# Ordering a two-layer diffusion kernel's instructions by a replay on a timeline of engine stages

## The chip, the cores and the metric

The kernel runs on one core of a Trainium2 chip. The metric is the device time of one execution in microseconds (us); lower is better.

## The reference, cut to what matters

Two layers over 256 latent tokens and 256 context tokens of width 1024. Each layer is a half-step SwiGLU, a token mixer, and another half-step SwiGLU, all modulated by nine vectors that come from the conditioning vector through one wide weight (`ada`). The even mixer is a bidirectional RWKV-7 recurrence over 12 heads beside a Fourier mix; the odd mixer is a convolution module beside pooling.

```python
def half_ffn(h, m, off, g, w_gu, w_down):
    y = modulate(h, g, m[off], m[off + 1])
    return h + 0.5 * m[off + 2] * swiglu(y, w_gu, w_down)

    def step(S, inp):
        rt, wt, kt, vt, kkt, bt = inp
        sk = jnp.einsum('bhij,bhj->bhi', S, kkt)
        S = S * wt[:, :, None, :] - sk[..., None] * bt[:, :, None, :] + vt[..., None] * kt[:, :, None, :]
        return S, jnp.einsum('bhij,bhj->bhi', S, rt)
```

## The kernel before, in words

The kernel computes everything on tiles with the channel on the 128 partitions. A product at full precision is split into high and low parts, three matmuls per tile (`mm3`, lines 195 to 197), or two where the moving operand holds both parts (lines 446, 447); VectorE and ScalarE split the weights (lines 190, 191).

The stages, with their place in the profiled execution:

- 0 to 405 us: setup and the first half feed-forward of layer 0 for both streams (`ffn`). The products of its start are ordered by hand (`manual_schedule`), nothing after it is.
- 405 to 858 us: the even mixer. `even_in` multiplies by the input weight, `shift` mixes neighbouring tokens. The heads are worked on in three groups, G0, G1 and G2. A group first has its `features` (decays and keys), then its `inverse` of 32x32 triangular blocks: a transpose on VectorE (line 697), 30 dependent pairs of a product and a subtraction on VectorE (lines 706, 708), two more transposes (713, 718), and two sets of 128 small matmuls (lines 727 and 738) which I call INV1 and INV2. Then its `chain` runs: eight dependent steps, each of which has a preparation that depends on nothing of the step before (products `pg`, lines 783 and 786, and transposes, line 805).
- While the chain of G0 runs, the features and the inverse of G1 run beside it; while that of G1 runs, those of G2; beside that of G2 runs the output projection (`fouriers`, `project_most`).
- 858 to 883 us: the rest of the projection (`project_last`). Then two feed-forwards (`half_ffn`, to 1080 and to 1265 us), the odd mixer (to 1400 us) and the last feed-forward.

Beside the chains lies a filler, `ada_wide` (lines 245 to 271): the modulation vectors of layer 1, in 18 blocks. A block loads four tiles `wraw` of 512 KB from a pool of four buffers, runs eight matmuls of 32 columns (line 260) into a bank called `ada`, then four transposes (line 268) and a reduction (line 269). Nothing in the even mixer needs its result. `drive(wide, PR[1 + g])` says how many of its pieces stand in the program beside a step of a chain.

No order of the work after the start is written out. The kernel is built by a tile scheduler: each engine works off one queue in order, and the scheduler, while it replays the program on a model of the machine, lays at each engine's queue whichever ready instruction has the best priority. The priority is the place in the program, moved by what the kernel asks: the filler's matmuls stand in `high_priority(-200)`, so they are taken when little else is ready. What is ready at which moment is the model's answer, so the model sets the order of each queue.

## Time and profile before

| what | value |
|---|---|
| median of three runs | 1593.63 us (1588.56 to 1593.87) |
| profiled execution, its own time | 1594.17 us |
| its span, first to last instruction | 1592.5 us |
| mean granted TensorE clock, share of full speed | 0.954 |
| TensorE (PE) busy | 1483.9 us, 93% |
| VectorE (DVE) busy | 1092.9 us, 69% |
| ScalarE (ACT) busy | 707.8 us |
| GpSimd (POOL) busy | 202.5 us |

Busy times are sums of the intervals in which an engine worked. Two engines can both be far from idle in the whole and each be the limit of some stage, so the table is only a start: a stage is read by itself, by the busy times in that stretch and by the chain of waits that crosses it. In rows of line 260 the trace holds two records for one matmul; eight records are four matmuls.

### The profile page before, as it was taken

How to read it: one execution, taken by the hardware profiler on the slowest of the kernel's cores; microseconds unless marked ns; L12 is line 12 of the kernel's file. 1: busy time of each engine (PE TensorE's matmuls, PEld its weight loads, DVE VectorE, ACT ScalarE, POOL GpSimd, SP SyncE). 2: the span in 40 equal slices, each digit the busy share in tenths (PEclk: the TensorE clock that was granted, in tenths of full speed). 3: DMA queues.
4: the chain of work that ended last, by engine and by line, in shares of the span. 5: the costliest groups of instructions: out<-in, count | busy, mean ns of one | idle time of the engine just before them, and what ended most of it. 6: DMA issues, size and time to landing. Idle time of an engine off the chain costs nothing.

```text
span 1592.5 us, 27107 instructions
## 1 busy us (share of the span) xinstructions
PE 1483.9 (93%) x10680; PEld 1207.1 (76%) x10680; DVE 1092.9 (69%) x1943; ACT 707.8 (44%) x1245; POOL 202.5 (13%) x293
## 2 busy tenths in 40 slices
PE   5999999999989979999898899999999986899997
PEld 3788888888877755445586788898888875888886
DVE  4799963334689688578365776667666499777764
ACT  3432222222454462542452655545554355555542
POOL 0000100000132141330211000000000066200000
PEclk9999999999999879899898999999999998799999
DMA  9766953332322124565531566665666432446663
GB/s 367 242 231 236 342 199 97 99 86 87 122 88 79 33 101 173 164 191 186 173 121 42 156 189 189 183 196 159 187 192 184 143 116 80 133 135 195 184 183 98
DMA packets 69312, 253.22 MB, mean 159 GB/s; under 512 B 8032, under 2 KB 11888, under 8 KB 64448
## 3 DMA queue, kind: packets, MB, share of 16 engines
q1 hardware_dynamic: 64592, 219.46, 44.1%
q0 software_dynamic: 4592, 32.03, 5.7%
q8 instruction: 84, 1.38, 0.4%
q14 instruction: 44, 0.36, 0.1%
HBM read 249.36 MB, written 2.10 MB: 158 GB/s over the span
## 4 chain that ended last, share of the span: by engine, by line
PE 79%; DVE 14%; ACT 3%; issue 2%; POOL 1%; DMA 1%; SPq 0%; POOLq 0%; DVEq 0%; ACTq 0%
PE gu L446 13%; PE down L446 7%; PE gu L447 7%; PE gu L195 6%; PE gu L196 6%; PE gu L197 6%; PE ada L260 4%; PE down L195 3%; PE down L196 3%; PE down L197 3%; PE down L447 3%; DVE wlo L191 2%; PE gu L1095 2%; DVE ocv L1068 2%; DVE oo L1068 1%
## 5 line engine op out<-in xcount | busy, mean ns | idle before, releaser
L190 ACT CAST whi<-wraw 128x1024 fp32r<-128x1024 f32 (+2 forms) x298 | 304.2, 1026 | 484.4 <-PE gu L196 150.6
L191 DVE TENSOR_TENSOR wlo<-wraw,whi 128x1024 fp32r<-128x1024 f32 (+2 forms) x298 | 356.2, 1199 | 203.3 <-ACT whi L190 196.1
L446 PE MATMUL gu<-yy,whi 128*128 128x512 f32 x960 | 333.9, 395 | 5.4 <-DVE yy L377 4.0
L447 PE MATMUL gu<-yy,wlo 128*128 128x256 f32 x960 | 264.2, 277 | 0.0
L446 PEld LDWEIGHTS gu<-yy,whi 128*128 128x128 f32 x960 | 179.2, 188 | 49.0 <-DVE yy L377 7.0
L447 PEld LDWEIGHTS gu<-yy,wlo 128*128 128x128 f32 x960 | 180.2, 188 | 1.0
L195 PE MATMUL gu<-yh,whi 128*128 128x512 f32 (+1 forms) x448 | 168.2, 377 | 6.2 <-ACT yh L375 4.3
L196 PE MATMUL gu<-yl,whi 128*128 128x512 f32 (+1 forms) x448 | 167.8, 375 | 0.0
L197 PE MATMUL gu<-yh,wlo 128*128 128x512 f32 (+1 forms) x448 | 167.3, 374 | 0.0
L446 PE MATMUL down<-hx,whi 128*128 128x512 f32 x462 | 160.3, 394 | 0.0
L447 PE MATMUL down<-hx,wlo 128*128 128x256 f32 x462 | 128.0, 277 | 0.0
L350 POOL TENSOR_TENSOR rs<-ms,mhalf 128x2 f32<-128x2 f32 (+1 forms) x9 | 10.9, 1209 | 815.9 <-DVE ms L347 625.5
L195 PEld LDWEIGHTS gu<-yh,whi 128*128 128x128 f32 x448 | 86.3, 193 | 24.1 <-ACT yh L375 5.6
L446 PEld LDWEIGHTS down<-hx,whi 128*128 128x128 f32 x462 | 86.6, 188 | 20.1
L281 DVE SCALAR_TENSOR_TENSOR adaj<-adaw,cb 128x1024 f32<-128x1024 f32 x80 | 97.7, 1222 | 5.7 <-DMA adaw<-in_adat_dram 4.6
L196 PEld LDWEIGHTS gu<-yl,whi 128*128 128x128 f32 x448 | 86.7, 194 | 15.1 <-DVE yl L377 1.0
L197 PEld LDWEIGHTS gu<-yh,wlo 128*128 128x128 f32 x448 | 86.7, 194 | 14.9 <-DVE wlo L191 0.8
L447 PEld LDWEIGHTS down<-hx,wlo 128*128 128x128 f32 x462 | 86.7, 188 | 0.0
L260 PE MATMUL ada<-wraw,ccs 128*32 128x512 f32 x288 | 74.1, 638 | 0.7 <-DMA wraw<-in_ada_dram 0.5
L384 DVE SCALAR_TENSOR_TENSOR hlat<-down,mc,hlat 128x256 f32<-128x256 f32 x67 | 32.4, 483 | 57.9 <-PE down L197 50.3
L196 PE MATMUL down<-hl,whi 128*128 128x512 f32 (+1 forms) x176 | 67.9, 386 | 0.0
L195 PE MATMUL down<-hh,whi 128*128 128x512 f32 (+1 forms) x176 | 67.9, 386 | 0.0
(362 smaller groups left out, 2760.2 us busy)
## 6 DMA issues: line engine op xcount, KB each, us to landing
wraw<-in_gu_dram SPq DMA_DIRECT2D x176, 512.0 KB, 3.9
wraw<-in_ada_dram SPq DMA_DIRECT2D x72, 512.0 KB, 4.5
adaw<-in_adat_dram POOLq DMA_DIRECT2D x28, 1024.0 KB, 6.1
wraw<-in_down_dram SPq DMA_DIRECT2D x56, 512.0 KB, 3.5
wraw<-in_win_dram SPq DMA_DIRECT2D x22, 512.0 KB, 3.5
wraw<-in_down_dram SPq DMA_DIRECT2D x24, 384.0 KB, 3.2
wraw<-in_down_dram SPq DMA_DIRECT2D x16, 448.0 KB, 3.3
wraw<-in_owin_dram SPq DMA_DIRECT2D x14, 512.0 KB, 3.5
```

The source lines that it names most:

```text
L190: nc.scalar.copy(hi[:, :k, :], raw[:, :k, :])
L191: (eng or nc.vector).tensor_tensor(out=lo[:, :k, :], in0=raw[:, :k, :], in1=hi[:, :k, :].bitcast(F32), op=ALU.subtract)
L195: mm(ps, lhsT=wh, rhs=xh, start=start, stop=False, **k)
L196: mm(ps, lhsT=wh, rhs=xl, start=False, stop=False, **k)
L197: mm(ps, lhsT=wl, rhs=xh, start=False, stop=stop, **k)
L260: nc.tensor.matmul(ps[32 * g:32 * g + 32, :], lhsT=self.cs[:, k, :], rhs=w[:, i, :], start=k < 4, stop=k >= 4, tile_position=(0, 32 * g), ...
L281: nc.vector.scalar_tensor_tensor(out=junk, in0=w[:, i, :], scalar=1.0, in1=self.cb[v], op0=ALU.mult, op1=ALU.mult, accum_out=self.mod[0, v ...
L384: nc.vector.scalar_tensor_tensor(out=h[v][:, k, :], in0=ps[:, n * T:n * T + T], scalar=gate[v][:, k:k + 1], in1=h[v][:, k, :], op0=ALU.mul ...
L446: mm(ps, lhsT=wh, rhs=x.rearrange("p s t -> p (s t)"), start=start, stop=False, skip_group_check=True)
L447: mm(ps[:, :T], lhsT=wl, rhs=x[:, 0, :], start=False, stop=stop, skip_group_check=True)
L1068: nc.vector.scalar_tensor_tensor(out=c, in0=u[:, w:w + T], scalar=cw[:, j, w:w + 1], in1=c, op0=ALU.mult, op1=ALU.add)
L1095: nc.tensor.matmul(ps[k // 2][:, k % 2 * T:k % 2 * T + T], lhsT=a[:, k, :], rhs=b[:, q, :], start=first and n == 0 and k % 2 == 0, stop=la ...
```

## The change

The kernel sets one environment variable before the framework is imported. The scheduler then replays the program on another model, a timeline of engine stages, and orders the queues by what is ready there. The program, its instructions, its tiles and its buffers stay the same; each line number grows by 3.

```diff
--- before.py
+++ after.py
@@ -1,6 +1,9 @@
+import os
 from contextlib import ExitStack
 
 import numpy as np
+
+os.environ["CONCOURSE_TILE_TIMELINE_SIM"] = "all"
 
 import concourse.bass as bass
 from concourse import mybir
```


What it does to the queues shows in their order. Three places follow. Line numbers are each kernel's own; `x2` and the like count equal neighbours.

TensorE at the first inverse, that of G0. `down_4493` is a product of `even_in`; `misc_4124` to `misc_4229` are INV1 and INV2 (lines 727 and 738 before, 730 and 741 after); `ada` is the filler. Before:

```order
L197 MATMUL down_4493<-yh_2979,wlo_4488 128x256
L727 MATMUL misc_4124<-Dt_4116,A_3319 32x32 x32
L727 MATMUL misc_4159<-Dt_4116,A_3319 32x32 x32
L195 MATMUL down_4493<-yh_2979,whi_4487 128x256
L196 MATMUL down_4493<-yl_2980,whi_4487 128x256
L197 MATMUL down_4493<-yh_2979,wlo_4488 128x256
L195 MATMUL down_4493<-yh_2979,whi_4487 128x256
L196 MATMUL down_4493<-yl_2980,whi_4487 128x256
L738 MATMUL misc_4194<-A_3319,R_716_4123 32x32 x32
L738 MATMUL misc_4229<-A_3319,R_716_4123 32x32 x32
L197 MATMUL down_4493<-yh_2979,wlo_4488 128x256
```

After:

```order
L271 MATMUL ada_5235<-cst,adas_5233 128x128 x4
L263 MATMUL ada_5241<-wraw_5242,ccs 32x512 x2
L263 MATMUL ada_5241<-wraw_5246,ccs 32x512 x2
L263 MATMUL ada_5241<-wraw_5492,ccs 32x512 x2
L263 MATMUL ada_5241<-wraw_5496,ccs 32x512 x2
L271 MATMUL ada_5502<-cst,adas_5500 128x128 x4
L730 MATMUL misc_4124<-Dt_4116,A_3319 32x32 x32
L730 MATMUL misc_4159<-Dt_4116,A_3319 32x32 x32
L263 MATMUL ada_5508<-wraw_5509,ccs 32x512 x2
L263 MATMUL ada_5508<-wraw_5572,ccs 32x512 x2
L263 MATMUL ada_5508<-wraw_5576,ccs 32x512 x2
L741 MATMUL misc_4194<-A_3319,R_716_4123 32x32 x32
```

What remained of `even_in` stood around INV1 and INV2; now `even_in` is finished earlier, and blocks of the filler stand there, together with the first preparations of the chain of G0.

TensorE in the chain of G1, beside the inverse of G2. `mx_7231` and `down_7279` are steps of the chain, `pg_7311` a preparation. Before:

```order
L869 MATMUL mx_7231<-ar_4561,Xs_7130 64x64
L869 MATMUL mx_7231<-rs_7019,Xs_7130 64x64
L260 MATMUL ada_6958<-wraw_6967,ccs 32x512
L824 MATMUL down_7279<-XV_7163,AG_7180 64x64 x8
L786 MATMUL pg_7311<-ar_4561,bk_4557 128x128 x2
L786 MATMUL pg_7311<-ar_4561,bk_4558 128x128
L833 MATMUL down_7290<-RH_7288,A_4563 64x64 x8
```

After:

```order
L872 MATMUL mx_7231<-ar_4561,Xs_7130 64x64
L872 MATMUL mx_7231<-rs_7019,Xs_7130 64x64
L827 MATMUL down_7279<-XV_7163,AG_7180 64x64 x8
L789 MATMUL pg_7311<-ar_4561,bk_4557 128x128 x2
L789 MATMUL pg_7311<-ar_4561,bk_4558 128x128 x2
L789 MATMUL pg_7311<-ar_4561,bk_4559 128x128 x2
L789 MATMUL pg_7311<-ar_4561,bk_4560 128x128 x2
```

The filler's lone matmuls between the pieces of the chain are gone from here. In the whole kernel the 144 filler matmuls stood in 59 runs of neighbours, and now stand in 35. Counted in rounds of up to four neighbours there were 67 and are 48. The table says where they stand, with the number of chain steps and of preparations in the same stretch:

| stretch of the program | filler matmuls, rounds before | after | steps before, after | preparations before, after |
|---|---|---|---|---|
| inverse of G0 | 0, 0 | 30, 10 | 0, 0 | 0, 4 |
| features of G1 | 14, 6 | 32, 12 | 3, 4 | 5, 2 |
| inverse of G1 | 34, 14 | 50, 17 | 5, 4 | 7, 5 |
| features of G2 | 38, 18 | 32, 9 | 3, 3 | 1, 3 |
| inverse of G2 | 42, 21 | 0, 0 | 5, 5 | 7, 3 |
| chain of G2 | 16, 8 | 0, 0 | 8, 8 | 5, 7 |

TensorE at the start of the second feed-forward. `gu_8628` is a product with the raw rows, `misc_8543` spreads the reciprocal norm over the partitions, `gu_8670` and its like are the first products with the normalised rows `yy`. Before:

```order
L196 MATMUL gu_8628<-yl_8449,whi_8622 128x258
L197 MATMUL gu_8628<-yh_8448,wlo_8623 128x258
L446 MATMUL gu_8670<-yy_8454,whi_8664 128x512
L447 MATMUL gu_8670<-yy_8454,wlo_8665 128x256
L446 MATMUL gu_8670<-yy_8454,whi_8664 128x512
L447 MATMUL gu_8670<-yy_8454,wlo_8665 128x256
L446 MATMUL gu_8693<-yy_8454,whi_8687 128x512
L447 MATMUL gu_8693<-yy_8454,wlo_8688 128x256
L446 MATMUL gu_8693<-yy_8454,whi_8687 128x512
L447 MATMUL gu_8693<-yy_8454,wlo_8688 128x256
```

After:

```order
L198 MATMUL gu_8628<-yh_8448,whi_8622 128x258
L199 MATMUL gu_8628<-yl_8449,whi_8622 128x258
L200 MATMUL gu_8628<-yh_8448,wlo_8623 128x258
L449 MATMUL gu_8670<-yy_8454,whi_8664 128x512
L450 MATMUL gu_8670<-yy_8454,wlo_8665 128x256
L449 MATMUL gu_8693<-yy_8454,whi_8687 128x512
L450 MATMUL gu_8693<-yy_8454,wlo_8688 128x256
L449 MATMUL gu_8726<-yy_8454,whi_8720 128x512
L450 MATMUL gu_8726<-yy_8454,wlo_8721 128x256
L449 MATMUL gu_8749<-yy_8454,whi_8743 128x512
L450 MATMUL gu_8749<-yy_8454,wlo_8744 128x256
```

Two accumulators were worked on in turn, now four; and the spread, which stood 43 rows ahead of the first `yy` product, stands 12 ahead, behind most of the raw products. At the next feed-forward it moves from 45 rows ahead to 21, at the last from 45 to 1.

On SyncE, which issues the loads, the order is nearly the same. On VectorE, the 60 dependent operations of an inverse have others between them: 18 before and 25 after in G0, 45 and 41 in G1, 45 and 27 in G2.

## Rows read from the trace of the kernel before

**Rows 1.** The page: busy time of each engine, share of the span, instructions.

```profile
PE 1483.9 (93%) x10680; PEld 1207.1 (76%) x10680; DVE 1092.9 (69%) x1943; ACT 707.8 (44%) x1245; POOL 202.5 (13%) x293
```

**Rows 2.** The page: the chain that ended last, by engine and by line.

```profile
PE 79%; DVE 14%; ACT 3%; issue 2%; POOL 1%; DMA 1%; SPq 0%; POOLq 0%; DVEq 0%; ACTq 0%
PE gu L446 13%; PE down L446 7%; PE gu L447 7%; PE gu L195 6%; PE gu L196 6%; PE gu L197 6%; PE ada L260 4%; PE down L195 3%; PE down L196 3%; PE down L197 3%; PE down L447 3%; DVE wlo L191 2%; PE gu L1095 2%; DVE ocv L1068 2%; DVE oo L1068 1%
```

**Rows 3.** Busy by stretch: length, PE, PEld, DVE, ACT, POOL, clock, DMA, GB/s.

```profile
443.00:492.00 49.00, 41.51 (x446) 33.95 (x446) 42.80 (x62) 27.70 (x44) 19.82 (x34) 0.90 0.18 60
492.00:545.60 53.60, 50.93 (x496) 45.35 (x495) 42.60 (x91) 20.56 (x29) 4.17 (x12) 0.90 0.25 77
545.60:593.40 47.80, 39.29 (x601) 27.43 (x599) 38.73 (x65) 29.31 (x54) 23.92 (x37) 0.84 0.25 85
593.40:644.50 51.10, 49.19 (x584) 29.59 (x582) 44.27 (x114) 15.48 (x38) 7.31 (x11) 0.92 0.51 173
644.50:706.70 62.20, 57.14 (x847) 30.77 (x848) 36.62 (x67) 30.89 (x54) 23.90 (x32) 0.86 0.50 157
706.70:761.30 54.60, 50.56 (x572) 27.57 (x572) 43.35 (x112) 16.53 (x38) 7.88 (x12) 1.00 0.62 198
761.30:858.00 96.70, 90.95 (x1134) 70.15 (x1135) 50.47 (x104) 41.45 (x83) 19.37 (x23) 0.93 0.37 117
858.00:883.00 25.00, 19.62 (x98) 13.72 (x98) 13.92 (x34) 10.43 (x22) 3.48 (x4) 0.73 0.36 108
```

**Rows 4.** The same view for line 260 alone: length, PE, PEld, clock, DMA, GB/s.

```profile
545.60:593.40 47.80, 5.91 (x28) 1.06 (x28) 0.84 0.25 85
593.40:644.50 51.10, 15.43 (x68) 2.20 (x68) 0.92 0.51 173
644.50:706.70 62.20, 22.65 (x78) 3.15 (x80) 0.86 0.50 157
706.70:761.30 54.60, 21.59 (x84) 3.11 (x84) 1.00 0.62 198
761.30:858.00 96.70, 8.48 (x32) 1.28 (x32) 0.93 0.37 117
```

**Rows 5.** Timeline of PE, end of the third inverse; start, us, engine, line, tiles.

```profile
751.17 1.04 PE L260 MATMUL ada<-wraw,ccs 128*32 128x512 f32 x2
...
757.29 1.06 PE L260 MATMUL ada<-wraw,ccs 128*32 128x512 f32 x8
...
761.35 0.82 PE L727 MATMUL misc<-Dt,A 32*32 32x32 f32 x40 [2.99 <-DVE Dt L718]
```

**Rows 6.** Groups by line, TensorE, 545 to 858 us: preparations of a chain step.

```profile
L786 PE MATMUL pg<-ar,bk 64*128 64x128 f32 x192 | 26.7, 323 | 0.0
...
L805 PE MATMUL mx<-cst,bk 128*128 128x128 f32 x84 | 17.4, 313 | 1.0 <-ACT UV L775 1.0
```

**Rows 7.** Timeline of VectorE, then of TensorE: first inverse.

```profile
490.31 1.96 DVE L697 STREAM_TRANSPOSE Y<-A 128x1024 f32<-128x1024 f32 x1
...
530.99 1.96 DVE L718 STREAM_TRANSPOSE Dt<-Z 128x1024 f32<-128x1024 f32 x1
...
533.00 3.30 PE L727 MATMUL misc<-Dt,A 32*32 32x32 f32 x128 [1.83 <-DVE Dt L718]
```

**Rows 8.** The page, DMA issues: median us from issue to landing; x72.

```profile
wraw<-in_ada_dram SPq DMA_DIRECT2D x72, 512.0 KB, 4.5
```

**Rows 9.** The chain of waits in features of group 1: start, us, what.

```profile
560.90 3.82 DMA wraw<-in_ada_dram
```

**Rows 10.** Timeline of TensorE, first feed-forward into the even mixer.

```profile
402.94 0.36 PE L195 MATMUL gu<-hh,whi 128*128 128x256 f32 x1
405.49 0.38 PE L356 MATMUL misc<-cst,rs 128*128 128x128 f32 x2
407.38 0.50 PE L195 MATMUL down<-yh,whi 128*128 128x256 f32 x2 [1.51 <-ACT yh L375]
```

**Rows 11.** Timeline of TensorE, start of the second feed-forward.

```profile
892.26 0.69 PE L356 MATMUL misc<-cst,rs 128*128 128x128 f32 x2 [1.38 <-POOL rs L350]
```

## The prediction, made before the changed kernel had run

> **What bounds the kernel now.** I read the page from the top, then the chain that ended last, then the busy times by stretch, and last the timelines of the places where the order changes. TensorE is busy for 93% of the span [rows 1], and the chain runs through it for 79% and through VectorE for 14% [rows 2]. So most of the kernel is a queue of products on TensorE. The feed-forwards are dense, and a new order of dense work can only touch their starts. The filler of the even mixer is different: it is on the chain for 4% [rows 2], some 64 us, though nothing near it needs its result. A new order can make that work cheaper or put it into idle time.
>
> The stretches show where idle time is [rows 3]. From 443 to 492 us TensorE works 41.51 of 49.00 us, from there to 545.6 us 50.93 of 53.60 us: 10.2 us idle. In the features of G1 (545.6 to 593.4) 8.5 us are idle. In the two inverses (593.4 to 644.5, 706.7 to 761.3) only 1.9 and 4.0 us are, and 15.4 and 21.6 us of TensorE's time there go to the filler [rows 4]. The reader is to see that the filler is done mostly where TensorE has little to spare.
>
> The price of the filler depends on its neighbours. A lone matmul of it takes 1.04 us, and four that stand together take 1.06 us [rows 5]: they write four column groups. The unit is therefore a round of up to four, at 1.05 us, not a matmul. The five stretches check this: the sum of their times, 74.1 us [rows 4], over 67 rounds is 1.1 us each.
>
> **The change, stage by stage.** No instruction is added or removed, so each term is idle time, shared rounds, or work that changes places. The counts are those of the table in the section on the change. Besides rounds, preparations of a chain step move. One has eight `pg` products, at 26.7 us for 24 preparations, and transposes, at 17.4 us for 21 [rows 6]: with the smaller products about 2.2 us, an estimate.
>
> *To the end of the first inverse, +11 us.* Ten rounds come here (10.5 us) and four preparations (8.8 us). The 10.2 us of idle time can take half of that. I add 2 us for filler tiles that have not landed when TensorE comes to them: a load takes 4.5 us from issue to landing [rows 8], and the first four blocks ask for sixteen. 10.5 + 8.8 + 2 - 10.2 is +11. The inverse itself runs on VectorE, 42.6 us from its first transpose to the end of its last [rows 7], and TensorE waits 1.83 us for it ahead of INV1. If all of the new work fits beside VectorE the term is near 0; if the idle time can't be filled it is +21.
>
> *Features of G1, 0.* Six rounds more (+6.3), three preparations fewer (-6.6). One chain step comes in, for which 8.5 us of idle time are there. Range -5 to +6.
>
> *Inverse of G1, -3 us.* Three rounds more (+3.2), two preparations fewer (-4.4), one step gone (about -2, taken near a preparation's 2.2). TensorE is full here [rows 3], so this is on the path. Range -5 to +2.
>
> *Features of G2, -8 us.* 18 rounds took 22.65 us [rows 4]; nine at 1.05 take 9.5 us: -13. Two preparations more: +4.4. TensorE is busy 57.1 of 62.2 us, so nearly all of it counts. Range -12 to -2.
>
> *Inverse of G2, -9 us.* All 21 rounds leave (-21.6), and four preparations (-8.8). TensorE would be left with about 20 of its 50.6 us, and then VectorE is late next: the inverse's dependent operations. The stretch is 54.6 us long; the inverse of G0, with 18 foreign operations between its dependent ones, took 42.6 us [rows 7]. So -12 is the most. With 27 foreign operations I take -9. If VectorE's operations are spaced by something else than TensorE's answers, 0.
>
> *Chain of G2, -4 us.* Eight rounds leave (-8.5), two preparations come (+4.4). TensorE is busy 91.0 of 96.7 us. Range -8 to 0.
>
> These give -13 us. The filler's cover is then gone from the last two stretches: what was hidden under it, the waits of the chain for VectorE and ScalarE, appears; that is why I gave these two less than TensorE's own account.
>
> *First feed-forward into the even mixer, +2.5 us.* Before, 21 products stand between the statistics and their spread, from 402.94 to 405.49 us, and still 1.51 us are waited for `yh` [rows 10]. Now the last statistics come after nearly all of these products. The cover of 2.5 us is lost. Range 0 to +4.
>
> *Starts of the feed-forwards, -3 us.* TensorE waits 1.38 us for the reciprocal norm, with raw products left that don't need it [rows 11]. They now go first, here and at the next feed-forward: twice -1.4. At the last one the spread moves behind all raw products, which can undo it; I take 0. Range -6 to +3.
>
> *The clock, +1.5 us.* The granted clock was 0.84 where TensorE was busy 39.29 of 47.80 us, and 1.00 where it was busy 50.56 of 54.60 [rows 3]. The inverse of G2 would become the emptier kind. About 20 us of work at 0.84 cost 3.8 us more than at 1.00; half of it lies under VectorE's time. The Trainium skill, "TensorE: Matmul & The Clock Gate", Part 1, states that the slow clock is the default and activity releases the full one, which speaks against a change that empties TensorE; the rows agree, and by that rule the whole stretch could fall to 1.2 GHz, which is the third rival below.
>
> *The odd mixer, 0.* The order on GpSimd and VectorE changes a little there; I found no wait that it removes, and bound it by -3 and +5.
>
> **Sum:** -13 + 2.5 - 3 + 1.5 = -12 us. Against the profiled execution's 1594.2 us that is **1582 us**. The median shown, 1593.6 us, is 0.6 us lower, which I leave out. 0.5%, 8 us, is about what a measurement of this kernel can tell from no change: faster means below 1585.6, slower above 1601.6.
>
> A second rule bears on the rounds. The rows show that a lone round between 64x64 products costs as much as one of four, 1.04 and 1.06 us. The Trainium skill, "TensorEngine Tiling (Array Packing)", Key Properties, states that changing the tiling mode drains TensorE. By that rule runs would count, 59 before and 35 now: at 74.1 us over 59, 1.26 us each, 24 fewer would give 30 us instead of 19 rounds times 1.05, 20 us; the sum would be 10 us lower, inside the range.
>
> **The rivals.** *VectorE sets the pace (about 1592 us).* The path of the even mixer from one inverse to the next is then the string of dependent operations on VectorE, and TensorE's saved rounds become waits. For it: VectorE is busy 44.27 of 51.10 us in the inverse of G1. Against it: TensorE is fuller, 49.19 us. Price: the work that moves ahead of the first inverse costs nothing then, and both later inverses give nothing. What stays is half of the -8 in the features of G2, some of the -4 in the last chain, and +1 of the other stages: 1594 - 2. It decides where the third inverse stays above some 52 us.
>
> *The filler is fed too slowly (about 1605 us, the slower side).* The 72 loads now are wanted between the first inverse and the features of G2, some 155 us instead of 250, and only four buffers exist. A matmul that waits for its tile holds TensorE's queue, and the chain step behind it. That this can happen is seen once: 3.82 us of the chain of waits is such a load [rows 9]. If six of the 18 blocks wait that long, it is +22.9 us: 1605. It decides from 12 us on, 0.7 us per block, and from 20 us, 1.1 per block, it would be seen as slower. For it: 18 blocks of 2.1 MB in 155 us are 244 GB/s, beside 60 to 77 GB/s of others, where these stretches had 198 at most [rows 3]. Against it: four buffers of 512 KB that land in 4.5 us [rows 8] could carry 466 GB/s. If each block waited 3.82 us it were +69 us; I hold that unlikely, since the filler is late only while it outruns its loads.
>
> *The clock falls (about 1588 us).* With the filler gone after the features of G2, TensorE goes through the inverse half idle, and the chain of G2 begins at 0.73, a mean between the levels of 1.2 and 2.4 GHz, as in the stretch from 858 to 883 us, which was 25.00 us long and 19.62 busy [rows 3], instead of 0.93. Over 20 us of work that is 20 x (0.93 / 0.73 - 1), +5.5 us.
>
> *The setting does nothing.* The order shows that it does; no chance.
>
> **How the numbers follow.** Forecast 0.58, own range 1563 to 1590 (the terms' bounds, not all at one end at once). VectorE 0.12, clock 0.08, slow feed 0.17, other 0.05. Faster: 0.52 of the forecast, 0.02 of the clock, 0.02 of the others: 0.56. Slower: 0.13 of the slow feed, 0.05 of VectorE, other mishaps and the early +11 growing to +21, 0.02 of the forecast's upper bounds and 0.01 of the clock: 0.21. The same: 0.23. The range takes the forecast's and most of the rivals' times: 1560 to 1606.
>
> **What would show it.** Line 263, which is line 260 now, should be busy near 50 us instead of 74.1, and not at all in the second half of G2's inverse. The first inverse should end about 11 us later, the third inverse be some 43 to 47 us long. In the chain of waits the filler's share should fall, and no piece of more than 1 us should be a load of `wraw` more than twice. It is wrong if the filler's busy time falls and the even mixer still ends at 858 us (VectorE), or if TensorE's idle time is released by loads of `wraw`.

## The result and the profile after

The changed kernel is slower by 0.6%: 1602.76 us, median of 12 runs (1590.58 to 1605.64), against 1590.72 us (12 runs, 1582.56 to 1594.99); ratio 1.0059, 95% interval 1.0041 to 1.0077 (the two medians are 0.8% apart). The forecast was 1582 us. The profiled execution took 1604.17 us (span 1602.5), 10.0 us more than that of before.

The page of the kernel after, busy times [rows 1] and the chain that ended last [rows 2]:

```profile
PE 1468.3 (92%) x10680; PEld 1209.1 (75%) x10680; DVE 1096.4 (68%) x1943; ACT 710.0 (44%) x1245; POOL 202.1 (13%) x293
...
PE 64%; DVE 17%; issue 14%; ACT 2%; DMA 1%; POOL 1%; SPq 0%; DVEq 0%; POOLq 0%; ACTq 0%
```

TensorE works 15.6 us less than before, as the change promised, and the kernel takes 10 us more. So about 26 us of waiting are new. Where they lie is seen with the same landmarks in both kernels: the spread of a reciprocal norm at the start of each stage.

| stretch | before | after | difference |
|---|---|---|---|
| start to the spread of the second feed-forward (end of the even mixer) | 892.26 | 889.12 | -3.14 |
| from there to the spread of the odd mixer (two feed-forwards) | 381.68 | 383.59 | +1.91 |
| odd mixer, to the spread of the last feed-forward | 126.01 | 136.42 | +10.41 |
| from there to the end of the execution | 194.22 | 195.04 | +0.82 |
| sum | 1594.17 | 1604.17 | +10.00 |

Single executions vary by some us in each line. The profiles of the experiments below show by how much, where a version leaves the order of a stage as it was. The even mixer ended at 885.9 and 892.3 us in the old order and between 886.5 and 893.7 us (five profiles) in the new one; the means are 889.1 and 889.6, so over such profiles there is no gain. The odd mixer's loss is beyond the variation, but its size is not fixed: 125.7 to 126.0 us in four profiles of the old order, 136.4 and 131.5 us in two of the new one.

The even mixer of the kernel after by stretch, columns as in [rows 3]. The cuts are the first transpose of an inverse and its INV1; the first cut is a plain time soon after the mixer's start, and the last row is the chain of G2:

```profile
409.60:503.40 93.80, 89.25 (x760) 78.22 (x759) 72.38 (x114) 50.22 (x78) 21.93 (x42) 0.97 0.27 83
503.40:549.80 46.40, 41.13 (x321) 29.78 (x321) 42.07 (x95) 18.87 (x30) 4.66 (x15) 1.00 0.52 167
549.80:609.90 60.10, 54.52 (x894) 33.69 (x895) 38.38 (x71) 31.77 (x58) 23.05 (x33) 0.86 0.54 188
609.90:657.10 47.20, 41.34 (x542) 22.72 (x541) 43.07 (x110) 15.95 (x36) 7.28 (x11) 1.00 0.72 249
657.10:716.60 59.50, 50.75 (x898) 33.75 (x898) 40.25 (x72) 33.68 (x61) 27.59 (x34) 0.89 0.48 168
716.60:760.40 43.80, 25.59 (x344) 22.02 (x346) 40.40 (x95) 11.91 (x26) 6.97 (x9) 0.61 0.08 25
760.40:889.10 128.70, 117.02 (x1341) 97.04 (x1342) 70.42 (x152) 55.95 (x113) 24.05 (x36) 0.84 0.23 73
sum 479.50, PE 419.59 PEld 317.21 DVE 346.97 ACT 218.35 POOL 115.55; mean PE 59.94 PEld 45.32 DVE 49.57 ACT 31.19 POOL 16.51
```

The sum line of the kernel before, cut at the same landmarks, from 408.0 us on:

```profile
sum 484.30, PE 440.84 PEld 317.56 DVE 345.07 ACT 216.54 POOL 114.67; mean PE 62.98 PEld 45.37 DVE 49.30 ACT 30.93 POOL 16.38
```

Read the two sums together: busy time fell by 21.3 us and the stretch by 4.8 (by 3.1, counted from the start of the execution). The idle time, length less busy, rose from 43.5 to 59.9 us. The row of the third inverse (716.60) holds 18.2 of it, where there were 4.0 before [rows 3]. TensorE is busy there for 25.59 of 43.80 us and VectorE for 40.40; the granted clock is 0.61, a mean between the two levels (1.2 and 2.4 GHz) and near the lower, where it was 1.00.

The filler by stretch, in the same cuts [rows 4]; three stretches are left out:

```profile
...
657.10:716.60 59.50, 12.37 (x64) 2.13 (x64) 0.89 0.48 168
716.60:760.40 43.80, 0.00 (x0) 0.00 (x0) 0.61 0.08 25
sum 257.00, PE 57.38 PEld 9.72; mean PE 11.48 PEld 1.94
```

57.38 us over 48 rounds is 1.2 us each; the rounds were saved, 16.7 us of them in time. What TensorE then waits for in the third inverse shows in the groups by line, TensorE, 717 to 769 us: `UV`, a step of the chain of G1 that VectorE has to answer, and TensorE waits 12.5 us for it.

```profile
L847 PE MATMUL down<-UV,BK 128*64 128x64 f32 x62 | 5.3, 300 | 12.5 <-DVE UV L839 11.5 <-ACT UV L838 1.0
```

The odd mixer is where the time was lost that no term of the forecast covered. Timelines of the kernel after, GpSimd and then TensorE, around its middle:

```profile
1358.65 9.89 POOL L194 TENSOR_TENSOR wm<-wraw,wm 128x1024 fp32r<-128x1024 f32 x4 [7.55 <-ACT wm L193]
1368.52 1.66 POOL L353 TENSOR_TENSOR rs<-ms,mhalf 128x2 f32<-128x2 f32 x1
```

```profile
1366.38 1.22 PE L1085 MATMUL misc<-osum,poolw 128*128 128x256 f32 x2 [3.80 <-DVE osum L1146]
1367.39 0.85 PE L1090 MATMUL down<-cst,osq 128*128 128x1 f32 x4
...
1374.44 0.63 PE L359 MATMUL misc<-cst,rs 128*128 128x128 f32 x2
```

The same on TensorE in the kernel before, where these lines are 1087, 1082 and 356:

```profile
1363.26 1.01 PE L1087 MATMUL down<-cst,osq 128*128 128x1 f32 x4 [2.57 <-ACT osq L1075]
...
1367.65 1.05 PE L1082 MATMUL misc<-osum,poolw 128*128 128x256 f32 x2
1368.50 0.63 PE L356 MATMUL misc<-cst,rs 128*128 128x128 f32 x2
```

The last statistics product (L1090), 0.85 us of work, now stands behind a pooling product that waits for VectorE; the reciprocal norm `rs` follows it, and its spread (L359) stands behind 24 products of the output mix that don't need it. All four weight subtractions are ahead of `rs` on GpSimd, where three were.

How much that costs varies with the same order. In one later version (two accumulators in turn, below) TensorE and GpSimd work through the odd mixer in exactly this order, and it takes 131.5 us. One operation of VectorE, and the stretch of the 24 products with columns as in [rows 3], in the kernel after and then in that version:

```profile
1358.71 2.61 DVE L1076 TENSOR_TENSOR oo<-oo,opart 128x256 f32<-128x256 f32 x1
1368.24:1374.44 6.20, 5.66 (x25) 5.36 (x25) 1.67 (x3) 0.31 (x1) 1.94 (x2) 0.50 0.64 219
```

```profile
1365.29 0.42 DVE L1094 TENSOR_TENSOR oo<-oo,opart 128x256 f32<-128x256 f32 x1
1372.00:1377.20 5.20, 3.38 (x25) 2.98 (x25) 4.21 (x4) 2.41 (x4) 5.14 (x3) 1.00 0.61 190
```

In the kernel after three operations of VectorE fall beside GpSimd's subtractions and take some 2.5 us each, in the other two; and its products run at a granted clock of 0.50, those of the other at 1.00. That is 2.2 us for the operation and 2.3 us for the products; added up, an estimate from these rows, nearly the whole difference of 4.9 us.

### The profile page after: what moved, and what is told of

Same layout as the page of the kernel before. It is cut to its first block, busy times and chain, and to the rows that moved or that the text cites. A ratio compares the mean times of both kernels' runs of the same rounds, so it can differ in the third digit from the quotient of the medians.

```text
span 1602.5 us, 27077 instructions
## 1 busy us (share of the span) xinstructions
PE 1468.3 (92%) x10680; PEld 1209.1 (75%) x10680; DVE 1096.4 (68%) x1943; ACT 710.0 (44%) x1245; POOL 202.1 (13%) x293
## 4 chain that ended last, share of the span: by engine, by line
PE 64%; DVE 17%; issue 14%; ACT 2%; DMA 1%; POOL 1%; SPq 0%; DVEq 0%; POOLq 0%; ACTq 0%
PE gu L449 9%; PE gu L198 6%; PE gu L199 6%; PE gu L200 6%; PE gu L450 5%; PE down L449 4%; PE down L198 3%; PE down L199 3%; PE down L200 3%; PE down L450 2%; DVE ocv L1071 2%; PE ada L263 2%; DVE oo L1071 2%; PE gu L1098 1%; DVE wlo L194 1%
## 5 line engine op out<-in xcount | busy, mean ns | idle before, releaser
L449 PE MATMUL gu<-yy,whi 128*128 128x512 f32 x960 | 343.4, 402 | 13.5 <-DVE yy L380 9.6
L450 PE MATMUL gu<-yy,wlo 128*128 128x256 f32 x960 | 271.0, 282 | 0.0
L449 PEld LDWEIGHTS down<-hx,whi 128*128 128x128 f32 x462 | 86.5, 188 | 20.5
L199 PEld LDWEIGHTS gu<-yl,whi 128*128 128x128 f32 x448 | 84.6, 189 | 14.9 <-DVE yl L380 1.0
L200 PE MATMUL down<-hh,wlo 128*128 128x512 f32 (+1 forms) x176 | 67.9, 386 | 0.0
```

The costliest lines, as they stand in the source:

```text
L199: mm(ps, lhsT=wh, rhs=xl, start=False, stop=False, **k)
L200: mm(ps, lhsT=wl, rhs=xh, start=False, stop=stop, **k)
L449: mm(ps, lhsT=wh, rhs=x.rearrange("p s t -> p (s t)"), start=start, stop=False, skip_group_check=True)
L450: mm(ps[:, :T], lhsT=wl, rhs=x[:, 0, :], start=False, stop=stop, skip_group_check=True)
```

## The experiments

### The odd mixer: three pins

Changed kernel; in the odd mixer the statistics go ahead of the second pooling product, `rs` ahead of the last two weight subtractions, the spread ahead of the second block of mix products. `issue_after` and `behind` set an order and add no wait.

```diff
+        for j, sq in enumerate(sqs):
+            for i in range(2):
+                st = nc.tensor.matmul(pst[:, i:i + 1], lhsT=sq[:, i * P:(i + 1) * P], rhs=self.ones,
...
+            if i:
+                self.behind(st, mm)
...
+                with self.tc.issue_after(self.rs_last.ins) if n > 5 else ExitStack():
+                    self.weight_into(wh, wl, ins["owout"][q], 0, nc.gpsimd)
...
+                with self.tc.issue_after(self.spread_last.ins) if n == 1 else ExitStack():
```

> The changed kernel with three orders pinned in the odd mixer: the last statistics product ahead of the last pooling product (TensorE), the reciprocal norm ahead of the last two weight subtractions (GpSimd), the spread ahead of the second block of output products (TensorE). Theory A: the stretch from the spread at the odd mixer's start to the first yy product of the last feed-forward grew from 133.2 to 141.8 us because these three stand behind work that could wait; then the stretch comes to about 135 us and the whole is some 7 us under the changed kernel, about 1596 us. Rival: VectorE sets that stretch, by its three operations of 2.5 us beside GpSimd; then it stays at 141 to 142 us, and the whole at about 1603.

Measured: 1598.59 us (12 runs), ratio to before 1.0032 (1.0015 to 1.0050). The stretch of the expectation is 138.4 us, neither theory A's 135 nor the rival's 141. The middle spread comes 92.4 us after the mixer's start (101.7 in the changed kernel, 94.6 before), but the mixer still takes 133.0 us, since from there to the last spread it is 40.6 us instead of 34.7 (31.5 before). TensorE in this kernel:

```profile
1361.40 0.43 PE L363 MATMUL misc<-cst,rs 128*128 128x128 f32 x2 [0.16 <-POOL rs L357]
1362.94 1.22 PE L1104 MATMUL gu<-oox,whi 128*128 128x256 f32 x4 [1.10 <-ACT oox L367]
1367.30 0.58 PE L1104 MATMUL gu<-oox,whi 128*128 128x256 f32 x1 [3.13 <-DVE oox L368]
```

The spread is early, and the next thing is late: `oox`, from VectorE. In the five profiles without these pins, all with the changed order here or nearly so, the middle spread came after 97.5 to 102.4 us, so the three places do set the first part. For the whole mixer no gain is shown: 133.0 us lies among the 131.5 to 137 us of those five, and the version with 131.5 us had a ratio of 1.0029.

### The odd mixer: two more pins

The kernel with three pins; the raw products of the last feed-forward behind the mixer's last product:

```diff
+                with self.tc.issue_after(self.mix_last.ins) if w == 3 else ExitStack():
+                    self.mm3(ps[:, :m], wh[:, k, :], wl[:, k, :], yh[:, k, :m], yl[:, k, :m], k == 0, k == KT - 1)
```

> The version with three pins in the odd mixer (1598.6 us, 133.0 us from the spread at its start to that of the last feed-forward), with one more: the raw products of the last feed-forward stand behind the last product of the odd mixer, as in the kernel before. Without it nine of the mixer's last products stand behind ten raw ones, and from the first update to the last statistics it takes 16.6 us instead of 13.4. Theory A2 (that is the second half of the odd mixer's loss): 129 to 130.5 us, total 1594 to 1597 us. Rival (the raw products only fill a wait of TensorE for the last weights): 132.5 to 134 us, total as it was, 1597 to 1601 us.

and besides, `rs` ahead of one subtraction only (`n > 6` for `n > 5`):

> As the version with the raw products held back, and the reciprocal norm of the odd mixer stands on GpSimd ahead of the last weight subtraction only, as in the kernel before, not ahead of the last two. Theory A3 (with two subtractions behind it, VectorE's conversion of a weight runs beside one and takes 2.64 us instead of 1.23, and TensorE waits 3.13 us for what is queued behind it): 126 to 128 us, total 1591 to 1595 us, which is the kernel before within what can be measured. Rival (the reciprocal is simply 2.4 us later): the same as or up to 2.4 us above the version with the raw products held back.

Measured: 1597.33 us (ratio 1.0008, 0.9988 to 1.0028) and 1598.08 us (1.0026, 1.0006 to 1.0047), both 12 runs. By the spreads the mixer takes 132.7 and 132.9 us. Both rivals hold, and A2 and A3 fall as single causes. In the first, the time from the first update to the last statistics did shrink, from 16.6 to 14.9 us; but the nine last products now wait for a bank that VectorE has to empty, and behind the last statistics the small operation on VectorE ahead of the reciprocal waits for a weight conversion (1397.76 to 1398.99 us):

```profile
1390.01 1.34 PE L1105 MATMUL gu<-oox,wm 128*128 128x256 f32 x9 [1.51 <-DVE hlat L391]
1396.95 0.28 PE L342 MATMUL misc<-cst,acc 128*128 128x1 f32 x2
...
1402.30 0.38 PE L363 MATMUL misc<-cst,rs 128*128 128x128 f32 x2
```

From the last statistics to the spread it is 5.35 us here and 2.90 before (1397.05 to 1399.95). Each pin moved the wait to the next small operation. What is shown: the three places delay the middle spread, and a fourth and a fifth pin change nothing further in the whole. What stays open is what holds the rest of the loss; the lines on the same order above name two things that vary it, the operations beside GpSimd's subtractions and the clock.

### The order of the dense products

In the dense parts of the three last feed-forwards the mean interval from the start of a product of 512 columns to the next product (waits left out) was 231.7, 231.7 and 231.8 ns in the profile before and 236.1, 235.5 and 234.9 after, some 2 us per feed-forward. Theory: the order (two accumulators in turn, or four) sets it. First, the changed kernel with two in turn, as before:

```diff
+            if f == 2:
+                ws = [self.weight(self.ins["gu"][w, 2 + n // 2, n % 2]) for n in range(2)]
+                begun = [self.bank("gu") for _ in ws]
+                self.chained = True
+                for k in range(KT):
+                    for ps, (wh, wl) in zip(begun, ws):
+                        self.mm2(ps, wh[:, k, :], wl[:, k, :], y[:, k], k == 0, k == KT - 1)
```

> The changed kernel with the normalised gate and up products of the three last feed-forwards pinned in program order: two accumulators in turn for the first pair, then one after the other, as they stood before. Theory B: in the dense stretches a 512-column product is followed by the next one after 231 ns in the kernel before and after 237 ns in the changed one, some 1,100 pairs, 7 us in all, and the order of the products at the start of the stretch decides which of the two it is; then the interval is 231 ns again and the whole 5 to 7 us under the changed kernel, about 1597 us. Rival: the interval differs from run to run or from chip to chip; then 237 ns stay, and the whole is within 2 us of the changed kernel.

Then the kernel before with four (`range(4)`):

> The kernel before with the first normalised gate and up products of the three last feed-forwards pinned to four accumulators in turn, k by k, as the changed kernel has them. Theory B: the interval after a 512-column product becomes 237 ns through the dense stretches, and the whole 3 to 7 us longer than the kernel before, about 1596 us. Rival: 231 to 233 ns stay, and the whole is within 2 us of the kernel before, or shorter by what four accumulators hide of the wait for yy.

Measured: 1599.64 us (12 runs; 1.0029, 1.0008 to 1.0050), intervals 235.3, 236.5 and 236.5 ns in the three feed-forwards; and 1637.01 us (6 runs; 1.0259, 1.0231 to 1.0287), 236.1, 236.1 and 230.0 ns. One order gives both values within one execution, so the theory falls. So does the kernel with the rounds alone (below), whose feed-forwards have the order of before: 236.1, 231.7 and 231.7 ns. The +44 us of the second has another cause. In its three feed-forwards TensorE waits 35.3 us ahead of these products, where it waited 5.3 before; four accumulators in one fixed line wait at their head for every operand, while two in one line waited 13.0 us, about as in the changed kernel (13.5). The rest, some 17 us, is longer busy time. TensorE:

```profile
900.57 0.77 PE L451 MATMUL gu<-yy,whi 128*128 128x512 f32 x1 [5.62 <-DVE wb L506]
```

What sets the interval is open. With 474 such pairs in a feed-forward, 4 ns are about 2 us of it: part of the variation between executions.

### The rounds alone

The kernel before, with the filler's matmuls fixed in rounds of four; 45 rounds instead of 67. The edit asks for nothing else, but the scheduler lays other work of the even mixer anew as well: 377 of VectorE's 1943 instructions stand at another place of its queue.

```diff
+            for i in range(2 if q % 2 else 0):
+                for g in (2 * i, 2 * i + 1):
+                    k = 2 * (q - 1) + g
+                    with self.tc.high_priority(-200 if g == 0 else 300):
+                        m = nc.tensor.matmul(ps[32 * g:32 * g + 32, :], lhsT=self.cs[:, k, :], rhs=ws[k // 2][:, k % 2, :],
...
+                    if g:
+                        self.behind(last, m)
```

> The kernel before with the filler's matmuls pinned together, four column groups at a time where their tiles have landed: 45 rounds instead of 67, in about the same stretches. Theory C: a round of up to four is the unit and it lies on TensorE's path; then line 260 is busy about 50 us instead of 74.1 and the even mixer is 15 to 22 us shorter, the whole about 1573 us. Rival: the filler mostly stands in time that TensorE would have to wait for the features and the chain anyway (in the changed kernel the features of G2 lost some 9 us of filler and became 2.7 us shorter); then line 260 falls the same but the whole only by 3 to 8 us.

Measured: **1572.69 us** (4 runs, 1571.34 to 1577.06), ratio 0.9872 (0.9847 to 0.9896). Theory C holds, and the kernel beats both others. The stretches from the third inverse on, and the sum from the same landmarks as above:

```profile
699.10:746.90 47.80, 43.43 (x582) 26.73 (x578) 44.08 (x113) 19.00 (x42) 8.30 (x13) 1.00 0.68 241
746.90:871.80 124.90, 114.74 (x1262) 89.50 (x1262) 68.55 (x150) 54.50 (x110) 22.85 (x34) 0.88 0.34 110
sum 463.80, PE 420.38 PEld 314.17 DVE 340.74 ACT 217.02 POOL 113.14; mean PE 60.05 PEld 44.88 DVE 48.68 ACT 31.00 POOL 16.16
```

TensorE is as busy as in the changed kernel (420.4 and 419.6 us) and idle as long as in the kernel before (43.4 and 43.5 us). Here a saved round comes with a saved microsecond: the filler's line fell from 74.1 to 52.05 us, and the stretch by 20.5. What the other moves share in that is not separated. The filler still reaches through the third inverse (12.58 us of it there), and the clock there is 1.00.

### The late first inverse

The first inverse starts at 503.4 us instead of 490.3 [rows 7]. In the changed kernel the small products of G0's features stand behind blocks of mostly 20 to 40 products of `even_in`. Changed kernel, with three of those blocks behind the features' products:

```diff
+                first_of = {5: "wa_last", 9: "spread_kk", 11: "wa_last"}.get(i)
+                with tc.issue_after(getattr(net, first_of).ins) if first_of else ExitStack():
+                    ps = begun[i] if i < 4 else net.even_in(i, n * T, yh, yl)
```

> The changed kernel with three orders pinned on TensorE in the features of G0: the sixth, tenth and twelfth product of even_in stand behind the feature products that were there before them in the kernel before. Theory D: in the changed kernel the features of G0 end 11 to 13 us late (first inverse from 503.4 us instead of 490.3) because each of their few small products stands behind 18 to 48 products of even_in; the products that give way find room in the third inverse, where the changed kernel's TensorE waits 12.5 us for UV; then the first inverse starts near 491 us and the even mixer ends (spread of the second feed-forward, 889.1 us) 8 to 11 us earlier. Rival: the work only changes places; the first inverse starts as early, but the even mixer ends within 3 us of 889.

Measured: 1599.80 us (1.0029, 1.0008 to 1.0051). The inverse starts at 497.5 us, INV1 at 549.1 instead of 549.8, the second feed-forward at 885.6 (886.5 to 893.7 in the changed order). The 8 to 11 us of theory D are not there. The stretch to the inverse, and the inverse:

```profile
409.60:497.50 87.90, 77.48 (x681) 68.69 (x682) 66.80 (x106) 46.67 (x73) 23.77 (x40) 0.89 0.24 75
497.50:549.10 51.60, 50.99 (x339) 41.75 (x337) 42.96 (x95) 18.05 (x28) 4.03 (x15) 0.96 0.34 108
```

In the second row TensorE is busy for all but 0.6 us, and is the limit: the `even_in` work only changes places with the inverse. INV1 comes no earlier, so the late start of the inverse costs little by itself.

### No filler at all

Both kernels with the filler left out (`wide = []`, and its vectors set to zero), to see what it costs each.

> The kernel before without the filler: the modulation vectors of layer 1 are set to zero, neither loaded nor computed. Theory C: the filler lies on TensorE's path with most of its 74 us of rounds and 13 us of transposes; the even mixer ends 60 to 80 us earlier than at 892 us. Rival: much of it stands where TensorE would wait for VectorE; then 25 to 45 us.

> The changed kernel without the filler, with the same part left out. Theory E: the new order without the filler is itself longer in the even mixer, by 12 to 18 us, through the late features of G0, and the saved rounds only pay that back; then the even mixer of this kernel ends 12 to 18 us later than that of the kernel before without the filler. Rival: the order of the rest costs nothing and the saved rounds are worth little; then the two end within 4 us of one another.

Measured: 1584.32 us (9 runs; 0.9924, 0.9897 to 0.9952) and 1593.92 us (10 runs; 0.9997, 0.9973 to 1.0022). Leaving out 74 us of TensorE's work, and the transposes with it, saves 9 us of the even mixer, far less than either theory said. The inverse of G1, the features of G2, its inverse and its chain in the kernel before without filler:

```profile
599.90:647.20 47.30, 36.82 (x498) 29.50 (x497) 42.56 (x108) 16.88 (x38) 9.04 (x13) 0.71 0.02 4
647.20:704.40 57.20, 41.58 (x746) 33.19 (x748) 35.01 (x57) 27.37 (x49) 23.93 (x32) 0.68 0.01 2
704.40:758.80 54.40, 41.09 (x502) 32.98 (x500) 46.22 (x109) 18.45 (x39) 8.42 (x13) 0.63 0.11 33
758.80:883.10 124.30, 112.10 (x1199) 89.58 (x1199) 63.55 (x137) 48.07 (x101) 21.40 (x32) 0.83 0.22 67
```

The first three were at 0.92, 0.86 and 1.00 [rows 3] and are at 0.71, 0.68 and 0.63. The third inverse does 41.09 us of work where it did 50.6 with 21.59 us of filler: the same products take longer, and it still lasts 54.4 us. Whether the clock keeps it that long is not shown: VectorE is busy for 46.22 of these 54.4 us, and in the changed order the third inverse takes 43.6 to 43.8 us in five profiles although its clock is 0.54 in one, 0.61 in another and 0.65 in three. Over that range the clock does not set its length.

Without filler the even mixer ends at 883.1 us in the old order and at 879.7 in the new one, so the new order of everything else costs nothing there. In the profiled pair without filler, 3.1 us apart, the odd mixer is the stage that is longer, by 8.7 us (125.9 and 134.7); the way to the end of the even mixer is 3.4 us shorter, and so are the two feed-forwards together. The medians are 9.6 us apart.

### The filler in the third inverse

The last test asks whether the place of the filler sets the even mixer: the changed kernel, with the last six blocks of the filler held back behind the features of G2.

```diff
-                with self.tc.high_priority(-200):
+                with self.tc.high_priority(-200), self.tc.issue_after(self.wa_last.ins) if b > 11 else ExitStack():
```

> The changed kernel with the last six blocks of the filler (12 to 17) held behind the last product of the features of G2, so that about 17 rounds stand in the inverse of G2, where it had none and the granted clock was 0.61. Theory F (an emptied TensorE pays with its clock, so the filler is worth most where TensorE would wait): the clock of the third inverse rises to 0.9 or more; the stretch from INV1 of G1 to the inverse of G2 gets shorter from 59.5 us to 50 to 54, the third inverse longer from 43.8 to 45 to 48; the second feed-forward starts at 882 to 885 us instead of 889; total 1594 to 1598 us. Rival (the even mixer does not care where the filler stands, since the kernels without any filler ended it at 880 to 883): the clock rises as well, but what the features gain the third inverse loses; second feed-forward at 887 to 891, total 1600 to 1604 us.

Measured: 1601.0 us (12 runs; 1.0036, 1.0016 to 1.0056). The rival holds. Features of G2, inverse and chain:

```profile
660.20:720.50 60.30, 51.34 (x810) 37.97 (x812) 38.38 (x62) 31.74 (x56) 26.27 (x34) 0.68 0.06 19
720.50:769.60 49.10, 42.68 (x576) 25.18 (x576) 43.67 (x116) 19.09 (x40) 8.62 (x11) 0.98 0.75 261
769.60:888.60 119.00, 108.42 (x1233) 89.85 (x1234) 65.54 (x142) 51.78 (x106) 23.63 (x34) 0.87 0.26 79
```

The clock goes to 0.98 in the inverse, which takes 5.3 us longer, and the features, emptied of 7.7 us of filler, fall to 0.68 and are no shorter (60.3 and 59.5 us). The chain is 9.7 us shorter than in the profile of the changed kernel (6.2 us shorter than the shortest with the changed order), which is not explained, and the second feed-forward still starts at 888.6 us. With a block of filler taken out of the features, what is left there takes longer: 46.7 us of busy time instead of 38.4. So the place of the filler does not explain the changed kernel's even mixer; moving it as a block from one stretch to another pays nothing.

All versions in one table, the even mixer from 408.0 us (order of before) or 409.6 us (changed) to the spread of the second feed-forward (us; idle is length less busy):

| kernel | length | TensorE busy | idle | clock, whole kernel |
|---|---|---|---|---|
| before | 484.3 | 440.8 | 43.5 | 0.954 |
| changed | 479.5 | 419.6 | 59.9 | 0.945 |
| changed, filler held back | 479.0 | 426.1 | 52.9 | 0.948 |
| before, rounds of four | 463.8 | 420.4 | 43.4 | 0.955 |
| before, no filler | 475.1 | 398.4 | 76.7 | 0.923 |
| changed, no filler | 470.1 | 384.3 | 85.8 | 0.922 |

## Why the prediction was wrong

The direction was wrong. Against the profiled pair the forecast was -12 and the result +10, 22 us apart. The odd mixer holds 10.4 of them, the even mixer with its clock 5.9 (-9 forecast, -3.1 seen), the feed-forwards 5.7 (-3 forecast, +2.7 seen). Over all profiles with the same order the first two misses are nearly of a size: the odd mixer +8.1 on average, the even mixer +0.5 where -9 was forecast.

**The step that failed first is "The odd mixer, 0".** It said that no wait is removed there, and bounded the term by -3 and +5 from that. The order had shown what moved, and I looked there for waits that go, not for waits that come. A statistics product of 0.85 us behind a pooling product that waits 3.80 us, and a spread behind 24 products, are plain in the queue. The runs show +10.4 us in the pair and +5.5 in the other profile of the same order, and without filler +8.7. Three pins bring the middle spread from 97.5 us or more to 92.4, so these waits are real; one and two further pins show that no single place carries the loss, and no pin is shown to shorten the mixer as a whole. Its cause is in part open.

**The even mixer, term by term,** as averages over profiles with the same order (two before, five after):

- *To the end of the first inverse* with the first feed-forward: +18.2, forecast +13.5. The idle time I counted on did not take up the work: idle up to INV1 was 11.4 us before and 9.8 after.
- *Features and inverse of G1*: -1.9, forecast -3. Right.
- *Features of G2*: -0.3 (-2.7 in the pair), forecast -8. This is the mis-sized term. TensorE's busy time did fall, from 57.14 [rows 3] to 50.75 us; the stretch hardly did. "Nearly all of it counts" was the wrong sentence. With 4.68 us of filler left (held back) it still takes 60.3 us, with none 57.2. In the changed kernel the chain of waits of its last 18 us crosses ScalarE, VectorE and GpSimd and no product of TensorE: the features' own path came next. The clock seems to have a part too: the same old order took 62.2 us at 0.86 and 57.1 at 0.97.
- *Inverse of G2*: -10.9, forecast -9. Right, and by the reason given: VectorE, with 27 foreign operations instead of 45, is the limit, and TensorE waits 12.5 us for its `UV`.
- *Chain of G2*: -4.5, forecast -4. Right.

So four of five terms came within 5 us, and the sum, without the clock, still went from -10.5 to +0.5, as the two that missed most had the same sign.

**Starts of the feed-forwards, -3.** The term took a wait away and did not ask what comes in its place. TensorE of the kernel after, second feed-forward [rows 11]:

```profile
889.12 0.38 PE L359 MATMUL misc<-cst,rs 128*128 128x128 f32 x2
...
893.03 0.47 PE L449 MATMUL gu<-yy,whi 128*128 128x512 f32 x1 [2.21 <-DVE yy L380]
```

From the spread to the first `yy` product it was 8.1, 7.2 and 7.1 us, and is 3.9, 4.9 and 5.4; but that is mostly the spread itself, which now stands behind raw products that used to follow it. Counted from the last statistics product the first `yy` product comes after 8.5, 8.5 and 7.9 us instead of 10.3, 9.4 and 9.3, and the idle time of TensorE in it is 2.3, 2.2 and 5.1 us instead of 2.7, 1.4 and 1.4: the wait for the reciprocal became a wait for `yy`. A part of the shorter time is the speed of the products, since the same old order took 9.0 and 7.9 us at the first two starts of the kernel with rounds. The two feed-forwards as a whole did not gain: 382.8 us on average in the old order (three profiles), 382.5 in the new one (seven).

**The clock, +1.5, and the third rival.** Its mechanism came: 0.61 in the third inverse, 0.84 in the chain of G2 where it was 0.89. The price is inside the terms above, and no run isolates it; the chain of G2 took 128.8 us at 0.84 and 125.2 to 125.5 at 0.86 (three profiles of the same order). The Trainium skill, "TensorE: Matmul & The Clock Gate", Part 1, states that activity releases the full clock; the rows without filler (0.71, 0.68 and 0.63 instead of 0.92, 0.86 and 1.00) agree.

**The other rivals.** VectorE as the pace of the mixer is half right: the features of G2 gave nothing, the third inverse did. It was to be known by a third inverse above 52 us, and that took 43.8. The slow feed did not come: over 503 to 717 us the filler's matmuls waited 0.9 us for their tiles.

```profile
L263 PE MATMUL ada<-wraw,ccs 128*32 128x512 f32 x288 | 57.4, 676 | 6.1 <-DVE mod L272 5.0 <-DMA wraw<-in_ada_dram 0.9
```

The row shows a small wait I had not thought of: 5.0 us for the reduction `mod`, which empties the filler's bank.

**The price of a round was right,** and the result hides it. The rounds alone, asked for in the kernel before, saved 22 us of the filler's line and 20.5 us of the mixer. What the prediction should have asked of each stretch is not only how much TensorE is relieved, but whether it is still the limit once relieved, and at what clock.

## What to carry to other kernels

Where a new order is judged, look at the small operations that others wait for (statistics, a reciprocal, its spread) in every stage, not only in the stage with the most moved rows, and note what now stands ahead of each. Work saved on the busiest engine counts only in a stretch where that engine stays the limit: read the next engine's path there before you book it. Work that nobody waits for was cheapest here when it was merged into full rounds and left spread over the stretches, and leaving it out gained far less than its busy time. And before a gain of some us in a stage is believed, look how far that stage varies between profiles with the same order.

## What was not expected of the hardware

TensorE's filler nearly paid for itself: without its 74.1 us [rows 4] and its transposes the kernel took 0.9924 of the time, some 12 us less. The granted clock of the three stretches above fell to between 0.63 and 0.71; how much of the missing gain is the clock, and how much are waits that the filler had filled, no run separates.

A small operation on VectorE took six times as long beside a subtraction on GpSimd. The kernel before, VectorE, then GpSimd:

```profile
1360.19 2.56 DVE L1073 TENSOR_TENSOR oo<-oo,opart 128x256 f32<-128x256 f32 x1
1362.68 2.57 DVE L1142 TENSOR_TENSOR osum<-os,poolc 64x256 f32<-64x256 f32 x1
...
1365.96 0.42 DVE L1142 TENSOR_TENSOR osum<-os,poolc 64x256 f32<-64x256 f32 x1
```

```profile
1357.54 7.42 POOL L191 TENSOR_TENSOR wm<-wraw,wm 128x1024 fp32r<-128x1024 f32 x3 [4.67 <-ACT wm L190]
```

`osum` takes 2.57 us beside the third subtraction and 0.42 behind it: while GpSimd works through its subtractions, one two-input operation of VectorE passes per subtraction. The Trainium skill, "SBUF — State Buffer", SBUF: two separate sides, states that a VectorE operation with two inputs in SBUF and a GpSimd operation that reads SBUF hold a shared port pair one at a time, for a whole instruction; these rows agree. It makes the place of GpSimd's subtractions in the odd mixer a price of its own, which no order on TensorE's queue shows: one such operation more took 2.2 us longer in one of two profiles of the same order.
